# Attention weights times V on one core: register loops for the copying engines, and the last unit's product in two column parts

## The chip, the cores and the metric

One core of a Trainium2 chip. The metric is the device time of one execution in microseconds (us), median of the runs of a kernel. A profile's span is some 1.8 us shorter than the time of the same run (1057.4 against 1059.18 us for the kernel before), so spans are compared with spans and times with times.

## The reference

```python
# attn_weights: 8 x 12 x 1024 x 1024 float32, v: 8 x 12 x 1024 x 64 float32
np.einsum('bhqs,bhsd->bhqd', attn_weights, v).astype(np.float32)
```

96 heads, 403 MB of weights, each used once.

## The kernel before

The weights come in 48 *units* of 4 MB in bf16 (8 MB read in fp32: the page gives 427.82 MB read from HBM, which is the weights and V in fp32; a load writes `abf` in bf16, 4096 KB an issue). Units 0 to 45 hold half of each of four heads (a *quad*, two units); units 46 and 47 hold two heads each. In every unit TensorE transposes 16 groups `g` of weights into PSUM, VectorE and ScalarE copy them to `at`, TensorE multiplies them with V, and the product is copied to `ot`, transposed back, and copied to the output buffer. Two units are in flight (`abf[0]`, `abf[1]`); GpSimd queues a load as soon as the unit that held its buffer has been transposed. The stores of the last four full quads are held back until the last load has been queued (two of them, by GpSimd) or has landed (two, by SyncE).

TensorE runs a register loop already. VectorE and ScalarE are unrolled:

```python
            for n in range(NU):
                for g in range(G):
                    if on_dve(g) == dve:
                        eng.wait_ge(s_t[dve], n * per + count_of(g))
                        ins = copy(out=at[:, g]..., in_=bank[g % 4].bitcast(bf16))
                        # ... cut
                eng.wait_ge(s_m[e], n + 1)
                # ... cut
                copy(out=o, in_=x).then_inc(s_ot[e])
            back_copy(NU - 1, 1 - e).then_inc(s_fin[1 - e])
```

The last unit arrives in four quarters. The product of a pair of heads is done by row half: both heads of half 0, then both of half 1. Note where the wait for the last quarter stands:

```python
            for g in range(G):
                if g in starts:
                    pe.wait_ge(*s_piece[n, starts[g]])   # g == 12: the last quarter
                if t == 1 and g == 12:
                    wait_both(s_vbf, n + 1)
                    pair_half(t, 0)                      # needs groups 0 to 7 alone
                transpose_g(abf[t], g, n + 1)
                # ... cut
            for half in range(t, 2):
                pair_half(t, half)
        wait_both(s_ot, NU + 1)
        transpose_back()
```

## Time and profile before

| | before |
|---|---|
| time, median (lowest to highest) | 1059.76 us (1059.4 to 1059.97) |
| span of the profile | 1057.4 us |
| DMA share of a pair of units in mid-run (43.55 us) | 1.01 |
| VectorE, ScalarE busy in such a pair | 16.0, 16.4 us |
| landing of the last load to the end of the span | 17.5 us |

The prediction shows the lines behind these numbers: the slices, the windows of a pair of units, the chain of work in order of time, and the windows of the end. Two more lines of the page of before are from the table of DMA queues; the columns are packets, MB, and the share of 16 engines' span:

```profile
q8 instruction: 4, 0.07, 0.0%
q14 instruction: 10, 0.08, 0.0%
```

The page labels both *instruction*, and I take them for the transfers that bring code to the engines while the kernel runs. They are 14 in all, of 8 KB each in queue 14 (0.08 MB over 10) and 16 KB in queue 8 (0.07 MB over 4).

### The profile page before, as it was taken

The page shows a single profiled execution, that of the slowest core. Times are in us where ns is not written, and L with a number is a line of the kernel's source. Part 1 is how long each engine was busy: PE and PEld are TensorE (multiplying, and loading weights), DVE is VectorE, ACT ScalarE, POOL GpSimd, SP SyncE. Part 2 cuts the span into 40 slices and gives each one's busy share as a digit, 9 for nine tenths or more (in the row PEclk, how much of TensorE's full clock was granted, in tenths as well). Part 3 has the DMA queues.
Part 4 walks back from the last instruction along what each step waited for, and adds up shares of the span by engine and source line. Part 5 has one row for each costly group of instructions (what it writes and reads, how often), then busy time and mean ns, then how long its engine had stood idle before and what let it go on. Part 6 is the DMA issues. An engine that isn't in the chain of part 4 may idle for free.

```text
span 1057.4 us, 15231 instructions
## 1 busy us (share of the span) xinstructions
PE 756.6 (72%) x6856; PEld 703.3 (67%) x6856; DVE 387.6 (37%) x582; ACT 394.1 (37%) x480; POOL 54.0 (5%) x105
## 2 busy tenths in 40 slices
PE   0876686856877668776687677776767668676796
PEld 0776586756866667666677576775767658676784
DVE  1443343423443234333353333433344334332443
ACT  0443343433443234333343333433344334433453
POOL 1000000000000000000000000000000000000010
PEclk9988888988889788888898878888788888888899
DMA  9999999999999999999999999999999999999997
GB/s 218 219 219 208 243 232 218 234 210 240 238 218 238 216 238 238 218 236 226 223 236 214 237 236 217 238 218 238 237 218 238 205 242 238 213 215 217 217 212 251
DMA packets 14958, 239.75 MB, mean 227 GB/s; under 512 B 1632, under 2 KB 2144, under 8 KB 5216
## 3 DMA queue, kind: packets, MB, share of 16 engines
q0 software_dynamic: 13824, 235.41, 99.2%
q1 hardware_dynamic: 1120, 4.19, 1.0%
q8 instruction: 4, 0.07, 0.0%
q14 instruction: 10, 0.08, 0.0%
HBM read 427.82 MB, written 25.17 MB: 428 GB/s over the span
## 4 chain that ended last, share of the span: by engine, by line
DMA 76%; PE 22%; issue 1%; POOL 0%; DVE 0%; ACT 0%; POOLq 0%; SPq 0%
DMA abf<-in_attn_weights_dram 76%; PE bank L127 22%; PE bank L169 1%; POOL abf L328 0%; PE bank L154 0%; DVE at L286 0%; DVE osb_last L265 0%; ACT ot L306 0%; POOLq L427 0%; SPq L77 0%
## 5 line engine op out<-in xcount | busy, mean ns | idle before, releaser
L127 PE MATMUL bank<-ident,abf 128*128 128x128 f32 x3072 | 466.6, 325 | 262.0 <-DMA abf<-in_attn_weights_dram 261.9
L127 PEld LDWEIGHTS bank<-ident,abf 128*128 128x128 f32 x3072 | 457.1, 215 | 275.3 <-DMA abf<-in_attn_weights_dram 274.3
L286 DVE COPY at<-bank 128x1024 bf16<-128x1024 bf16 x480 | 319.8, 688 | 498.6 <-PE bank L127 497.1
L286 ACT COPY at<-bank 128x1024 bf16<-128x1024 bf16 x288 | 289.1, 1012 | 440.4 <-PE bank L127 440.4
L169 PE MATMUL bank<-at,vbf 128*64 128x256 bf16 (+1 forms) x3008 | 220.2, 280 | 2.1 <-DMA abf<-in_attn_weights_dram 1.3
L169 PEld LDWEIGHTS bank<-at,vbf 128*64 128x64 bf16 x3008 | 194.9, 108 | 21.8 <-DVE at L286 4.8
L306 ACT COPY ot<-bank 128x512 f32<-128x512 f32 x48 | 28.1, 585 | 184.5 <-PE bank L169 184.5
L306 DVE COPY ot<-bank 128x512 f32<-128x512 f32 x48 | 33.2, 691 | 152.2 <-PE bank L169 152.2
L154 PE MATMUL bank<-ident,ot 128*128 128x128 f32 x392 | 52.2, 276 | 31.6 <-DVE vbf L251 30.9
L328 POOL DMA_DIRECT2D abf<-in_attn_weights_dram x52 | 27.7, 533 | 896.2 <-PE bank L127 895.2
L154 PEld LDWEIGHTS bank<-ident,ot 128*128 128x128 f32 x392 | 43.3, 141 | 44.3 <-DVE vbf L251 42.2
L265 ACT COPY osb<-bank 128x512 f32<-128x512 f32 x92 | 49.4, 589 | 19.9 <-PE bank L154 19.9
L251 DVE CAST vbf<-bank 128x512 bf16<-128x512 f32 x48 | 31.0, 686 | 7.3 <-PE bank L142 7.3
L251 ACT CAST vbf<-bank 128x512 bf16<-128x512 f32 x48 | 25.9, 588 | 11.9 <-PE bank L142 11.9
L142 PE MATMUL bank<-vr,spread 32*128 32x512 bf16 x384 | 26.7, 377 | 0.0
L142 PEld LDWEIGHTS bank<-vr,spread 32*128 32x128 bf16 x384 | 10.2, 92 | 7.3
L340 POOL DMA_DIRECT2D out_dram<-osb x21 | 11.3, 540 | 41.7 <-ACT osb L265 41.7
L333 POOL DMA_DIRECT2D vr<-in_v_dram x23 | 12.1, 527 | 19.2 <-PE bank L142 18.9
L315 DVE CAST vr<-v 128x2048 bf16<-128x2048 f32 x1 | 1.5, 1498 | 3.2 <-DMA v<-in_v_dram 3.2
L361 POOL TENSOR_SCALAR_AFFINE_SELECT spread<-spread 32x512 bf16<-32x512 bf16 x4 | 2.5, 628 | 0.6
L265 ACT COPY osb_last<-bank 128x512 f32<-128x512 f32 x3 | 1.7, 587 | 0.8 <-PE bank L154 0.8
L265 DVE COPY osb_last<-bank 128x512 f32<-128x512 f32 x1 | 0.7, 690 | 2.9 <-PE bank L154 2.9
(9 smaller groups left out, 3.4 us busy)
## 6 DMA issues: line engine op xcount, KB each, us to landing
abf<-in_attn_weights_dram POOLq DMA_DIRECT2D x46, 4096.0 KB, 33.3
out_dram<-osb POOLq DMA_DIRECT2D x21, 1024.0 KB, 34.3
vr<-in_v_dram POOLq DMA_DIRECT2D x23, 512.0 KB, 34.5
abf<-in_attn_weights_dram POOLq DMA_DIRECT2D x2, 2048.0 KB, 26.3
abf<-in_attn_weights_dram POOLq DMA_DIRECT2D x4, 1024.0 KB, 22.9
out_dram<-osb SPq DMA_DIRECT2D x2, 1024.0 KB, 7.5
v<-in_v_dram SPq DMA_DIRECT2D x1, 1024.0 KB, 4.8
out_dram<-osb_last SPq DMA_DIRECT2D x1, 512.0 KB, 10.2
```

The source lines that it names most:

```text
L127: last = pe.matmul(out=pt[g % 4][:, k], lhsT=words[:, k], rhs=ident, is_transpose=True, start=(k == 0), stop=(k == KW - 1),)
L142: last = pe.matmul(out=ps, lhsT=spread[rows, b], rhs=vr[rows, b], start=(b == 0), stop=(b == VB - 1),)
L154: last = pe.matmul(out=px[k][:, ds(j * P, P)], lhsT=ot[:, 4 * k + j], rhs=ident, is_transpose=True, start=(j == 0), stop=(j == 3),)
L169: last = pe.matmul(out=outs, lhsT=vbf[:, 2 * kw + par, h], rhs=at[:, ds(half * GH, GH), kw, ds(col * np_, np_), par], start=(n == 0), stop ...
L251: copy(out=vbf[:, :, h], in_=ps.rearrange("p (k d) -> p k d", k=SB)).then_inc(s_vbf[e])
L265: return copy(out=halves[:, :, ds(4 * k, 4)].rearrange("p half j d -> p j half d"), in_=px[k].rearrange("p (j half d) -> p j half d", half ...
L286: ins = copy(out=at[:, g].rearrange("c k j two -> c (k j two)"), in_=bank[g % 4].bitcast(bf16),)
L306: copy(out=o, in_=x).then_inc(s_ot[e])
L328: pool.dma_start(out=abf[n % 2][:, ds(g0, gn)].rearrange("p g s -> p (g s)"), in_=in_).then_inc(s_abf[n % 2] if k == 0 else s_piece[n, k][ ...
L333: pool.dma_start(out=vr.rearrange("p b x -> p (b x)"), in_=v_g[iv]).then_inc(s_v, 16)
L340: eng.dma_start(out=out_q[q], in_=osb[q % NO].rearrange("p r d -> p (r d)"), **({} if by_sync else {"single_packet": True}),).then_inc(s_e ...
L361: pool.affine_select(out=spread[ds(h * VP, VP)], in_=spread[ds(h * VP, VP)], compare_op=mybir.AluOpType.not_equal, fill=1.0, base=0, patte ...
```

## The change

Its parts: (a) VectorE and ScalarE run register loops, of two and four units; (b) for these, the output buffers in the loop are two that alternate, and SyncE passes on to ScalarE, as `s_free`, which is free; (c) the products of the two last units are ordered by head, with the row half changing inside; (d) the last unit's product is done in two column parts (groups 0 to 3 and 8 to 11, then 4 to 7 and 12 to 15), each over both row halves, each transposed back and copied by itself; (e) the last quarter is loaded in two pieces, five loads in all. The diff, cut to its core:

```diff
-        NU - 1: [(0, 4), (4, 4), (8, 4), (12, 4)],
+        NU - 1: [(0, 4), (4, 4), (8, 4), (12, 2), (14, 2)],
 ...
-        def pair_half(t, half):
+        def multiply_pair(t, j0, jn):
             for h in range(2):
-                last = multiply(po[h][ds(half * D, D)], 2 * t + h, half, HP, h)
-                if half == 1:
-                    last.then_inc(s_m[h])
+                for half in range(2):
+                    outs = po[h][ds(half * D, D), ds(j0 * HP, jn * HP)]
+                    last = multiply(outs, 2 * t + h, half, HP, h, j0, jn)
+                last.then_inc(s_m[h])
 ...
+                if t == 1 and g == 12:
+                    wait_both(s_vbf, n + 1)
+                    wait_both(s_cp[10:12], n + 1)
+                    multiply_pair(t, 0, 4)
                 if g in starts:
                     pe.wait_ge(*s_piece[n, starts[g]])
-                if t == 1 and g == 12:
-                    wait_both(s_vbf, n + 1)
-                    pair_half(t, 0)
 ...
-        transpose_back()
+        transpose_back([(0, 4, px[0])])
+        wait_both(s_last, NU)
+        multiply_pair(1, 4, 4)
+        wait_both(s_ot, NU + 2)
+        transpose_back([(4, 2, px[1]), (6, 2, bank[0])])
 ...
-            for n in range(NU):
+            un, iters = (2, LOOPED) if dve else (4, BY_EIGHTS)
+            with nc.Fori(1, iters + 1, 1, engines=(DVE if dve else ACT,)) as it:
+                base = [eng.snap(it * (un * k) - un * k) for k in (per, 1, 2, 1)]
+                of_free = None if dve else eng.snap(it * 2 - 2)
+                for n in range(un):
+                    rows = osb[(n - 1) // 2 % 2][:, ds((n - 1) % 2 * G, G)]
+                    unit(n, base, rows, of_free + (n + 1) // 2 if n % 2 == 1 and not dve else None)
 ...
+            if 0 < q <= 2 * (BY_EIGHTS - 1):
+                nc.sync.wait_ge(s_osb[slot(q - 1)], 16 * ((q - 1) // 2 + 1))
+                nc.sync.sem_inc(s_free)
```

More of the change, by code (lines that the diff above doesn't have):

```diff
@@ L32 @@
     bf16 = mybir.dt.bfloat16
-    PE = mybir.EngineType.PE
+    PE, DVE, ACT = (getattr(mybir.EngineType, x) for x in ("PE", "DVE", "Activation"))
     B, H, Q, S = attn_weights.shape
@@ L54, with slot @@
     BY_SYNC = HELD_FROM + 2
-    NO = HELD + 2
+    BY_EIGHTS = HELD_FROM // 2
+    NO = 2 + LOOPED - 2 * BY_EIGHTS
     pieces_of = {
         NU - 2: [(0, GH), (GH, GH)],
-        NU - 1: [(0, 4), (4, 4), (8, 4), (12, 4)],
+        NU - 1: [(0, 4), (4, 4), (8, 4), (12, 2), (14, 2)],
     }
+    def slot(q):
+        return q % 2 if q < 2 * BY_EIGHTS else q - 2 * BY_EIGHTS + 2
     attn_q = attn_weights.rearrange("b (hq four) (p r) s -> (b hq) (four p) (r s)", four=VH, p=VP)
@@ L117 @@
         s_memset, s_const, s_vr = sem("s_memset"), sem("s_const"), sem("s_vr")
+        s_free = sem("s_free")
         pe = nc.tensor
@@ L149, in spread_v, with transpose_back @@
                 last.then_inc(s_sp[h % 2])
-        def transpose_back():
-            for k in range(2):
-                for j in range(4):
+        def transpose_back(parts=((0, 4, px[0]), (4, 4, px[1]))):
+            for j0, jn, ps in parts:
+                for j in range(jn):
                     last = pe.matmul(
-                        out=px[k][:, ds(j * P, P)],
-                        lhsT=ot[:, 4 * k + j],
+                        out=ps[:, ds(j * P, P)],
+                        lhsT=ot[:, j0 + j],
                         rhs=ident,
@@ L159, in transpose_back, with multiply @@
                         start=(j == 0),
-                        stop=(j == 3),
+                        stop=(j == jn - 1),
                     )
                 last.then_inc(s_back)
-        def multiply(outs, h, half, np_, col):
+        def multiply(outs, h, half, np_, col, j0=0, jn=GH):
             n = 0
@@ L171, in multiply @@
                         lhsT=vbf[:, 2 * kw + par, h],
-                        rhs=at[:, ds(half * GH, GH), kw, ds(col * np_, np_), par],
+                        rhs=at[:, ds(half * GH + j0, jn), kw, ds(col * np_, np_), par],
                         start=(n == 0),
@@ L232 @@
                 wait_both(s_vbf, n + 1)
-            wait_both(s_last, n + 1)
-            for half in range(t, 2):
-                pair_half(t, half)
+                wait_both(s_last, n + 1)
+                multiply_pair(t, 0, GH)
         wait_both(s_ot, NU + 1)
-        transpose_back()
+        transpose_back([(0, 4, px[0])])
[3 more added lines that the diff above has]
+        transpose_back([(4, 2, px[1]), (6, 2, bank[0])])
         def engine(dve):
@@ L244, in engine, with spread_copy @@
             e = 0 if dve else 1
-            spreads = 0
-            def spread_copy(h, ps):
-                nonlocal spreads
-                spreads += 1
-                eng.wait_ge(s_sp[e], spreads)
+            def spread_copy(h, ps, count):
+                eng.wait_ge(s_sp[e], count)
                 copy(
@@ L253, in spread_copy @@
                 ).then_inc(s_vbf[e])
-            def back_copy(n, k):
-                if n < NU - 2:
-                    if n % 2 == 0 and k == 0 and n // 2 >= NO:
-                        eng.wait_ge(s_osb[n // 2 % NO], 16 * (n // 2 // NO))
-                    rows = osb[n // 2 % NO][:, ds(n % 2 * G, G)]
-                else:
-                    rows = osb_last[n % 2]
-                halves = rows.rearrange("p (half j) d -> p half j d", half=2)
-                eng.wait_ge(s_back, 2 * (n + 1) + k + 1)
-                return copy(
-                    out=halves[:, :, ds(4 * k, 4)].rearrange("p half j d -> p j half d"),
-                    in_=px[k].rearrange("p (j half d) -> p j half d", half=2, d=D),
-                )
@@ L270, in middle @@
-            def middle(n):
-                if n < NU - 2:
-                    if n % 2 == 0:
-                        spread_copy(e, po[e])
-                        spread_copy(2 + e, px[e])
-                else:
-                    spread_copy(2 * (n % 2) + e, po[e])
-                if not dve and n > 0:
-                    back_copy(n - 1, 0)
-                    back_copy(n - 1, 1).then_inc(s_out)
-            for n in range(NU):
-                for g in range(G):
-                    if on_dve(g) == dve:
-                        eng.wait_ge(s_t[dve], n * per + count_of(g))
-                        ins = copy(
-                            out=at[:, g].rearrange("c k j two -> c (k j two)"),
-                            in_=bank[g % 4].bitcast(bf16),
-                        )
-                        if g < G - 4:
-                            ins.then_inc(s_cp[g])
-                        elif g == (G - 1 if dve else G - 2):
-                            ins.then_inc(s_last[e])
-                    if g == 3 and n == NU - 1:
-                        middle(n)
-                if n < NU - 1:
-                    middle(n)
-                eng.wait_ge(s_m[e], n + 1)
-                if n < NU - 2:
-                    o = ot.rearrange("c j (h p) -> c h j p", h=VH)[:, ds(2 * e, 2)]
-                    x = po[e].rearrange("c (h j p) -> c h j p", h=2, j=GH)
-                else:
-                    o = ot.rearrange("c j (h p) -> c h j p", h=2)[:, e]
-                    x = po[e].rearrange("c (j p) -> c j p", j=GH)
-                copy(out=o, in_=x).then_inc(s_ot[e])
@@ L307, in engine, with back_copy, rows_of @@
-            back_copy(NU - 1, 1 - e).then_inc(s_fin[1 - e])
+            def back_copy(rows, j0, jn, ps, count):
+                eng.wait_ge(s_back, count)
+                return copy(
+                    out=rows.rearrange("p (half j) d -> p j half d", half=2)[:, ds(j0, jn)],
+                    in_=ps[:, ds(0, jn * P)].rearrange("p (j half d) -> p j half d", half=2, d=D),
+                )
+            def rows_of(n):
+                if n < NU - 2:
+                    return osb[slot(n // 2)][:, ds(n % 2 * G, G)]
+                return osb_last[n % 2]
@@ new lines, in back_copies, with copy_g @@
+            def back_copies(rows, count, free=None):
+                if free is not None:
+                    eng.wait_ge(s_free, free)
+                for k in range(2):
+                    last = back_copy(rows, 4 * k, 4, px[k], count + k + 1)
+                last.then_inc(s_out)
+            def copy_g(g, count):
+                eng.wait_ge(s_t[dve], count)
+                ins = copy(
+                    out=at[:, g].rearrange("c k j two -> c (k j two)"),
+                    in_=bank[g % 4].bitcast(bf16),
+                )
+                if g < G - 4:
+                    ins.then_inc(s_cp[g])
+                elif g == (G - 1 if dve else G - 2):
+                    ins.then_inc(s_last[e])
@@ new lines, in product_four, with product_pair @@
+            def product_four(count):
+                eng.wait_ge(s_m[e], count)
+                copy(
+                    out=ot.rearrange("c j (h p) -> c h j p", h=VH)[:, ds(2 * e, 2)],
+                    in_=po[e].rearrange("c (h j p) -> c h j p", h=2, j=GH),
+                ).then_inc(s_ot[e])
+            def product_pair(j0, jn, count):
+                eng.wait_ge(s_m[e], count)
+                copy(
+                    out=ot.rearrange("c j (h p) -> c h j p", h=2)[:, e, ds(j0, jn)],
+                    in_=po[e].rearrange("c (j p) -> c j p", j=GH)[:, ds(j0, jn)],
+                ).then_inc(s_ot[e])
@@ new lines, in engine, with unit @@
+            mine = [g for g in range(G) if on_dve(g) == dve]
+            def unit(n, base, rows, free):
+                of_t, of_sp, of_back, of_m = base
+                for g in mine:
+                    copy_g(g, of_t + (n * per + count_of(g)))
+                if n % 2 == 0:
+                    spread_copy(e, po[e], of_sp + (n + 1))
+                    spread_copy(2 + e, px[e], of_sp + (n + 2))
+                if not dve:
+                    back_copies(rows, of_back + 2 * n, free)
+                product_four(of_m + (n + 1))
@@ new lines, in engine @@
+            for n in range(un * iters, NU - 2):
+                unit(n, (0, 0, 0, 0), rows_of(n - 1), None)
+            for t in range(2):
+                n = NU - 2 + t
+                for g in mine:
+                    if t == 1 and g >= 12 and mine[mine.index(g) - 1] < 12:
+                        product_pair(0, 4, n + 1)
+                    copy_g(g, n * per + count_of(g))
+                    last = mine[-1] if t == 0 else [x for x in mine if x < 4][-1]
+                    if g == last:
+                        spread_copy(2 * t + e, po[e], n + 1)
+                        if not dve:
+                            back_copies(rows_of(n - 1), 2 * n)
+                if t == 0:
+                    product_pair(0, GH, n + 1)
@@ L309 @@
+            if not dve:
+                back_copy(rows_of(NU - 1), 0, 4, px[0], 2 * NU + 1).then_inc(s_fin[0])
+            product_pair(4, 4, NU + 1)
+            ps = px[1] if dve else bank[0]
+            back_copy(rows_of(NU - 1), 4 + 2 * e, 2, ps, 2 * NU + 2 + e).then_inc(s_fin[1])
         nc.vector.memset(ident, 0.0).then_inc(s_memset)
@@ L338, in store @@
             eng = nc.sync if by_sync else pool
-            eng.wait_ge(s_out, 2 * q + 2)
+            eng.wait_ge(s_out, 2 * q + 3)
             eng.dma_start(
                 out=out_q[q],
-                in_=osb[q % NO].rearrange("p r d -> p (r d)"),
+                in_=osb[slot(q)].rearrange("p r d -> p (r d)"),
                 **({} if by_sync else {"single_packet": True}),
-            ).then_inc(s_end if by_sync else s_osb[q % NO], 16)
+            ).then_inc(s_end if by_sync else s_osb[slot(q)], 16)
         load_attn(0)
@@ L385 @@
         nc.sync.dma_start(out=v32.rearrange("p b x -> p (b x)"), in_=v_g[0]).then_inc(s_v0, 16)
-        for iv in range(1, NV):
-            nc.sync.wait_ge(s_v, 16 * iv)
+        nc.sync.sem_inc(s_free, 2)
+        for q in range(LOOPED):
+            nc.sync.wait_ge(s_v, 16 * (q + 1))
             nc.sync.sem_inc(s_vr)
+            if 0 < q <= 2 * (BY_EIGHTS - 1):
+                nc.sync.wait_ge(s_osb[slot(q - 1)], 16 * ((q - 1) // 2 + 1))
+                nc.sync.sem_inc(s_free)
         nc.sync.wait_ge(*s_piece[NU - 1, len(pieces_of[NU - 1]) - 1])
@@ L391 @@
             store(q, by_sync=True)
-        nc.sync.wait_ge(s_out, NU - 1)
+        nc.sync.wait_ge(s_out, NU)
         nc.sync.dma_start(out=out_p[NU - 2], in_=osb_last[0]).then_inc(s_end, 16)
         for k in range(2):
-            nc.sync.wait_ge(s_fin[k], 1)
+            nc.sync.wait_ge(s_fin[k], k + 1)
             gs = [x.rearrange("p (half g) d -> p half g d", half=2)[:, :, ds(4 * k, 4)]
@@ L398 @@
             nc.sync.dma_start(out=gs[0], in_=gs[1]).then_inc(s_end, 16)
-        for q in range(BY_SYNC - NO, BY_SYNC):
-            nc.sync.wait_ge(s_osb[q % NO], 16 * (q // NO + 1))
+        for q in range(2 * BY_EIGHTS - 2, BY_SYNC):
+            nc.sync.wait_ge(s_osb[slot(q)], 16 * BY_EIGHTS if q < 2 * BY_EIGHTS else 16)
         nc.sync.wait_ge(s_end, 16 * (LOOPED - BY_SYNC + 3))
```

## The prediction

> **What bounds the kernel now.** I read the page's slices and queue table first, then the chain of work in order of time, then windows of 43.55 us, then the timeline and the windows of the last 50 us.
>
> ```profile
> DMA  9999999999999999999999999999999999999997
> ...
> q0 software_dynamic: 13824, 235.41, 99.2%
> ...
> DMA 76%; PE 22%; issue 1%; POOL 0%; DVE 0%; ACT 0%; POOLq 0%; SPq 0%
> ```
>
> The first line is the mean busy share of the 16 DMA engines: 90% or more in every slice but the last. The second says that the queue of the loads alone fills 99.2% of the engines' span. The third, the chain that ended last, gives TensorE 22%, which looks like something to win. The windows, one for each pair of units, say it is not:
>
> ```profile
> 524.40:567.95 43.55, 31.64 (x290) 29.76 (x289) 16.02 (x24) 16.39 (x20) 2.12 (x4) 0.85 1.01 229
> ```
>
> In 43.55 us (two units) VectorE is busy 16.02 us, ScalarE 16.39 us, TensorE 31.64 us, and the DMA share is 1.01. The compute part of the chain is work beside a transfer already queued:
>
> ```profile
> 509.00 0.53 POOL L328 DMA_DIRECT2D abf<-in_attn_weights_dram  x1 [17.77 <-PE bank L127]
> ...
> 523.85 6.35 PE L127 MATMUL bank<-ident,abf 128*128 128x128 f32 x30 [7.30 <-DMA abf<-in_attn_weights_dram]
> ```
>
> The next load was queued at 509.00 and the one before it landed only at 523.85: transposes and copies could run some 15 us late before the DMA queue ran dry. So from about 2 us to the landing of the last load the time is bytes over DMA rate, and only the end can be won. The chain there:
>
> ```profile
> 1010.48 29.42 DMA abf<-in_attn_weights_dram
> 1039.94 3.80 PE bank L169 x16
> 1043.74 2.15 PE bank L127 x16
> 1045.91 0.70 DVE at L286
> 1046.66 3.81 PE bank L169 x16
> 1050.49 0.59 ACT ot L306
> 1051.09 0.14 issue
> 1051.22 1.08 PE bank L154 x8
> 1052.33 0.69 DVE osb_last L265
> ```
>
> The last quarter of the last unit lands at 1039.9. Only then does TensorE do the product of the first row half (3.80 us), which needs nothing of that quarter: it stands behind the wait in program order. Then come 16 transposes, a copy, the product of the second half, copy, transpose back, copy. The last two stores are issued at 1052.50 and 1053.15, and the span ends at 1057.4. From landing to end: 17.5 us.
>
> [...] in the timeline
>
> ```profile
> 1009.43 4.48 PE L169 MATMUL bank<-at,vbf 128*64 128x256 bf16 x64
> ...
> 1012.00 0.69 DVE L306 COPY ot<-bank 128x512 f32<-128x512 f32 x1 [2.65 <-PE bank L169]
> ...
> 1024.04 6.55 PE L169 MATMUL bank<-at,vbf 128*64 128x512 bf16 x32
> ```
>
> 64 products of 256 columns that change the column half every 8 take 4.48 us (70 ns each), while 32 of 512 columns, the same columns, that stay 16 long on one half take 6.55 us. Changing halves often is worth a third. [...]
>
> **The change, part by part.** *Register loops on VectorE and ScalarE.* They replace unrolled copies by the same copies with waits on registers: nearly one register operation for each of some 18 or 19 instructions a unit, and one branch for 2 units (VectorE) or 4 (ScalarE). [...] Two additional copies back in unit 0 (0.59 us each on ScalarE) also lie under the loads. Before the last two units nothing changes in bytes, in their order, or in how many stores are held back (2 issued by GpSimd, 2 by SyncE): 0 us.
>
> *Buffers of the output.* Two alternate in the loop in place of six. ScalarE now waits for the store of two quads (four heads) earlier. A store is issued about 10 us after a quad's first unit starts and lands after 34.3 us; its buffer is asked for some 65 us after that issue: 30 us to spare, 0 us.
>
> *Product of the last but one unit.* The order of its four runs of 8 now changes the half each time, 32 of 512 columns. The loop's pattern took 2.57 us (1009.43 to 1012.00) for 32 of 256, so about 5.1 us in place of 6.55: TensorE is free 1.4 us earlier, at 1029.1.
>
> *The last unit.* Its four loads were issued at 1008.92 to 1010.48 and landed after 16.4 to 29.4 us: 1025.3, 1030.2, 1035.0 and 1039.9, one each 4.87 us. The fourth becomes two: 1037.4 and, with all bytes the same, 1039.9 again. Groups 4 to 11 follow 1.4 us earlier (group 8 just meets its load at 1035.0), and the last copy of them ends at 1038.2 in place of 1039.65. The first column product no longer waits for a load: 1038.2 + 2.5 = 1040.7. Transposes of groups 12 to 15 start there; from their start to their last copy it was 2.93 us (1043.67 to 1046.60), so 1043.6. The four first transposes back fit in that gap. Second column product: 2.57 us to ScalarE's copy, 1046.2. That copy has 256 columns: ScalarE's 0.585 us for 512 and 1.01 for 1024 extrapolate to 0.37 (estimate), 1046.6. Then 0.15 of waiting, two and two transposes back and a copy of 256 columns, about 0.67 + 0.37: 1047.8. The last store is issued then, not at 1053.15: **the compute end moves by 5.3 us**: 3.8 of it are the product that no longer follows the landing, the rest the shorter product and copies, less a first column product that now delays groups 12 to 15 by 0.8.
>
> *What the stores make of it.* The other end does not move. Behind the last load stand four held stores of 1 MB and one of 0.5 MB:
>
> ```profile
> 1046.00:1048.00 2.00, 1.34 (x6) 0.68 (x7) 0.60 (x1) 0.44 (x1) 0.00 (x0) 1.00 0.97 406
> 1048.00:1050.00 2.00, 2.00 (x10) 0.97 (x9) 0.69 (x1) 0.00 (x0) 0.00 (x0) 1.00 0.32 131
> 1050.00:1052.00 2.00, 1.23 (x10) 0.81 (x8) 0.00 (x0) 0.70 (x2) 0.00 (x0) 1.00 0.02 8
> ```
>
> ```profile
> out_dram<-osb_last SPq DMA_DIRECT2D x1, 512.0 KB, 10.2
> out_dram<-osb_last SPq DMA_DIRECT2D x2, 256.0 KB, 2.6
> ```
>
> The last two numbers of each window are DMA share and GB/s: full until 1048, a few slow engines until 1050.4. The 512 KB store, issued at 1040.8, lands at 1051.0. In the old kernel the last two stores came to idle engines. In the new one they are ready at about 1044.3 and 1047.8 and stand behind that backlog. On the slowest engines it grows by both: they took 1.55 us together (1053.75 to 1055.3), so data end at about 1050.4 + 1.5 = 1051.9. From data end to the span's end it was 2.1 us: 1054.0. The compute path alone would give 1047.8 + 4.2 = 1052.0. The later counts: 1057.4 − 1054.0 = 3.4 us, and I take 3.7[...]. The time is then 1059.7 − 3.7 = **1056.0 us**.
>
> **Rivals.** *The compute end is the bound, and stores hide:* 1059.7 − 5.4 = 1054.3. For it: the mean backlog is gone by 1048.3, and only two or three engines are late. Against it: a store is done when its slowest engine is. *The loops hurt:* a late copy delays the transposes, these the loads. For it: waits on registers and a jump back at each turn. Against it: 15 us of slack and 37% busy engines. If a stall of a few us fell on each turn, still 0; only over 15 us would it show, as DMA shares below 0.95 in the 43.55 us windows, 1060 or more. *The output buffers stall:* with two in the loop, a store later by 30 us would stop ScalarE and then TensorE; each such stall costs what it exceeds the slack by; nothing in the landing times (34.0 median, 36.1 at most) points there. *Code fetch:* shorter programs for two engines save transfers, but the queues of kind instruction hold 14 packets, 0.15 MB of 239.75: below 0.6 us.
>
> **Range and chances.** The two ends give 1054.3 and 1056.3; half a us for landings, and more if the five loads slow the last landing or the two column products overlap less than in the loop: 1054.0 to 1057.8. Two per cent are 21 us, more than the whole end of 17.5: faster 0.01, same 0.98, slower 0.01.
>
> **What would show it.** In the new profile: DMA share still 1.00 and 43.55 us a pair in mid-run; the last load's landing near 1039.9; the first column product near 1038.2, before that landing; the second starting at 1043.6 and taking 2.5 us, not 3.8; the last store issued near 1047.8 with a landing of 4 us or so, not 2.6, if the backlog holds it, and about 2.6 if the compute end is the bound. Wrong would be: a pair longer than 43.6 us, ScalarE waiting for free output buffers, or a last landing moved by over 1 us.

What no trace of this case shows is cut from the recorded text, with the cuts marked; the part on the order of the matmuls therefore begins in mid-sentence. The sum came to 1059.7 − 3.7 = 1056.0 us: 0 for the loops, 0 for the buffers, 3.7 for the end. And the reason for taking 3.7 where 3.4 was worked out is gone; the 0.3 was my estimate, which no run shows. That a store is done when its slowest engine is, the profile of before shows: the 512 KB store lands at 1051.0, 2.7 us after the 1048.3 at which the prediction has the mean backlog gone, and in the last half us in which anything moves (1050.0 to 1050.5) the DMA share is 0.08.

## The result, and the profile after

1055.41 us median of 4 runs (1054.98 to 1056.07), against 1059.76 before: 4.35 us less; ratio 0.996, 95% interval 0.9943 to 0.9977. That is "the same" at 2%, clear of noise, and inside the predicted range.

The chain of work of the changed kernel in order of time, from unit 46's product on (columns: start us, us, what):

```profile
1023.84 4.74 PE bank L176 x32
...
1038.03 2.52 PE bank L176 x32
1040.56 2.13 PE bank L134 x16
...
1042.71 0.70 DVE at L287
...
1043.46 2.57 PE bank L176 x32
...
1046.05 0.38 ACT ot L306
...
1046.56 0.64 PE bank L161 x4
...
1047.23 0.37 ACT osb_last L268
```

There is no load in this part of the chain any more: compute is done at 1047.60, where the old kernel was done at 1053.02. That is 5.4 us, but the span is only 3.7 us shorter (1053.7 against 1057.4). The windows of the end show where the rest went. The columns are busy time by engine, granted clock, DMA share and GB/s, as in the three windows of before:

```profile
1046.00:1048.00 2.00, 0.64 (x5) 0.42 (x4) 0.42 (x1) 0.74 (x2) 0.00 (x0) 1.00 0.98 408
1048.00:1050.00 2.00, 0.00 (x0) 0.00 (x0) 0.00 (x0) 0.00 (x0) 0.00 (x0) 1.00 0.95 353
1050.00:1052.00 2.00, 0.00 (x0) 0.00 (x0) 0.00 (x0) 0.00 (x0) 0.00 (x0) 0.90 0.17 58
```

Every compute engine is idle from 1048 on, and the DMA engines are full until 1050 (share 0.95, where it was 0.32 before). The end has become a drain of stores. SyncE's timeline and its waits say the same from the other side:

```profile
1039.59 0.82 SPq L385 DMA_DIRECT2D out_dram<-osb  x2
...
1043.76 4.40 SPq L447 DMA_DIRECT2D out_dram<-osb_last  x2
```

```profile
SPq L450 <- DMA out_dram<-osb_last: 3.7, 1, 3.7
```

The first issue comes on the landing of the last load, at 1039.59. The last two stores are issued from 1043.76 on, the second one's issue ends at 1048.16, and SyncE then waits 3.7 us for the stores to land; in the old kernel that wait was 1.9 us:

```profile
SPq L401 <- DMA out_dram<-osb_last: 1.9, 1, 1.9
```

In mid-run nothing moved. The window of the same pair of units as before, and two lines of the page:

```profile
524.40:567.95 43.55, 31.22 (x290) 29.35 (x289) 16.02 (x24) 17.62 (x21) 2.12 (x4) 0.85 1.01 229
```

```profile
q14 instruction: 4, 0.03, 0.0%
...
L287 ACT ACT_TABLE_LOAD x9 | 11.5, 1283 | 1.2 <-SPq L83 1.1
```

The DMA share is 1.01 again, and VectorE has the same 16.02 us. ScalarE has 1.28 us more in every other pair: its function table is now loaded inside the loop, nine times, where the unrolled kernel loaded it once. And the code transfers in queue 14 fell from 10 to 4.

### The profile page after: what moved, and what is told of

Read it like the earlier page. It is cut to its first block, busy times and chain, and to the rows that moved or that the text cites. A ratio compares the mean times of both kernels' runs of the same rounds, so it can differ in the third digit from the quotient of the medians.

```text
span 1053.7 us, 16145 instructions
## 1 busy us (share of the span) xinstructions
PE 753.2 (71%) x6888; PEld 704.7 (67%) x6888; DVE 387.5 (37%) x583; ACT 404.9 (38%) x492; POOL 54.6 (5%) x106
## 4 chain that ended last, share of the span: by engine, by line
DMA 73%; PE 25%; issue 1%; ACT 0%; DVE 0%; POOL 0%; POOLq 0%; SPq 0%
DMA abf<-in_attn_weights_dram 73%; PE bank L134 23%; PE bank L176 1%; PE bank L161 0%; ACT at L287 0%; PE bank L149 0%; DVE at L287 0%; POOL abf L373 0%; ACT ot L306 0%; ACT osb_last L268 0%; POOLq L476 0%; SPq L83 0%
## 5 line engine op out<-in xcount | busy, mean ns | idle before, releaser
L176 PE MATMUL bank<-at,vbf 128*64 128x256 bf16 x3040 | 215.9, 279 | 1.5 <-ACT at L287 1.2
L268 ACT COPY osb<-bank 128x512 f32<-128x512 f32 x94 | 50.5, 589 | 20.8 <-PE bank L161 20.8
L287 ACT ACT_TABLE_LOAD x9 | 11.5, 1283 | 1.2 <-SPq L83 1.1
```

Source lines behind the costliest of these rows:

```text
L176: last = pe.matmul(out=outs, lhsT=vbf[:, 2 * kw + par, h], rhs=at[:, ds(half * GH + j0, jn), kw, ds(col * np_, np_), par], start=(n == 0), ...
L268: return copy(out=rows.rearrange("p (half j) d -> p j half d", half=2)[:, ds(j0, jn)], in_=ps[:, ds(0, jn * P)].rearrange("p (j half d) -> ...
L287: ins = copy(out=at[:, g].rearrange("c k j two -> c (k j two)"), in_=bank[g % 4].bitcast(bf16),)
```

## The experiments

All are timed beside the kernel before on the same chip; the last column is the median of the runs of before recorded with it less the run's own. E1 to e4 ran on one chip, c0 and e5 to e11 on another. "Changed kernel" is the one above, the *control* is its repetition c0_after. All are "the same" at 2% but e11, which is slower (ratio 1.0289).

| run | what | median us (range) | less than before |
|---|---|---|---|
| c0_after | the changed kernel again | 1055.68 (1055.4 to 1056.36) | 4.28 |
| e1_tail_only | new end alone | 1056.52 (1056.0 to 1057.2) | 3.11 |
| e2_loops_only | loops and buffers alone | 1058.95 (1058.84 to 1059.17) | 0.68 |
| e3_hoist | before, one wait moved | 1058.24 (1057.85 to 1058.47) | 1.39 |
| e4_four_loads | four loads, not five | 1055.55 (1055.18 to 1055.99) | 4.08 |
| e5_delay6 | six copies ahead of the last one | 1055.63 (1055.28 to 1055.96) | 4.33 |
| e6_delay11 | eleven copies ahead of it | 1058.37 (1057.93 to 1058.5) | 1.59 |
| e7_no_held | no held stores (wrong result) | 1053.45 (1053.35 to 1054.41) | 6.51 |
| e8_held5 | five held stores | 1055.82 (1055.29 to 1056.44) | 4.01 |
| e9_held3 | three held stores | 1056.21 (1055.9 to 1056.45) | 3.62 |
| e10_half_order | products in the old order | 1056.46 (1056.22 to 1056.86) | 3.37 |
| e11_pad | more code on SyncE | 1089.53 (1085.0 to 1093.52) | −29.7 |

**The change in two.** The new end without loops:

```diff
-            with nc.Fori(1, iters + 1, 1, engines=(DVE if dve else ACT,)) as it:
-                ...
+            for n in range(NU - 2):
+                ...    # the copies of before, unrolled
-    NO = 2 + LOOPED - 2 * BY_EIGHTS
+    NO = HELD + 2
```

> The changed kernel without the register loops and with the six output buffers of before: only the new end (column parts, order of the last-but-one product, five loads). My theory, that the loops and buffers are worth nothing and the end everything: 1055.4 us as the changed kernel, within 0.5. Rival, that the shorter programs of VectorE and ScalarE give part of the gain: 1056 to 1058 us.

The loops with the old end:

```diff
-        NU - 1: [(0, 4), (4, 4), (8, 4), (12, 2), (14, 2)],
+        NU - 1: [(0, 4), (4, 4), (8, 4), (12, 4)],
-                multiply_pair(...)
+                pair_half(...)     # and the rest of the end of before
```

> The register loops and the two alternating output buffers, with the end of before (four loads, products by row half). My theory: 1059.7 us as before, within 0.4, although the loop of ScalarE loads its function table 9 times (11.5 us in the changed kernel's profile). Rival, that loops cost or give something: 1058 or less, or 1061 or more.

The end alone gave 3.11 us, the loops and buffers alone 0.68. My theory ("worth nothing") missed both by more than it allowed; the loops and buffers do give a part, whatever its cause: all five runs of e1 are slower than all five of e4 (the changed kernel with four loads), by 0.97 in the median though by only 0.01 at the edges, and all five of e2 are faster than all nine of before. The interval of e2's ratio (0.998 to 1.0007) still holds 1, so e2 by itself would not settle it. The two parts sum to 3.8 us, against 4.1 for e4 and 4.3 for the control; what is left is inside the scatter of the changed kernel's own runs (1054.98 to 1056.36).

**One moved wait.** The smallest edit that takes the old product from behind the landing:

```diff
-                if g in starts:
-                    pe.wait_ge(*s_piece[n, starts[g]])
                 if t == 1 and g == 12:
                     wait_both(s_vbf, n + 1)
                     pair_half(t, 0)
+                if g in starts:
+                    pe.wait_ge(*s_piece[n, starts[g]])
```

> The kernel before with one edit: the product of the first row half stands ahead of the wait for the last quarter, not behind it. It can start at 1038.65, when the transposes of groups 8 to 11 end, in place of 1039.94, so the rest follows 1.3 us earlier; before, the stores had drained by 1050.4, so the compute end sets the time there: 1059.7 - 1.3 = 1058.4 us. If the 3.8 us of that product were all behind the landing for the wait alone: 1056 us.

1.39 us, as expected. In its timeline the product starts before the landing, which SyncE's issue marks:

```profile
1039.16 3.80 PE L169 MATMUL bank<-at,vbf 128*64 128x512 bf16 x16
...
1040.54 0.82 SPq L340 DMA_DIRECT2D out_dram<-osb  x2
```

The wait itself is thus worth 1.4 us: TensorE had only that much free time before the landing. The rest of the product's 3.8 us still holds up the last transposes.

**Four loads.**

```diff
-        NU - 1: [(0, 4), (4, 4), (8, 4), (12, 2), (14, 2)],
+        NU - 1: [(0, 4), (4, 4), (8, 4), (12, 4)],
```

> The changed kernel with the last quarter of the last unit as one load in place of two. TensorE is busy with the first column product until 1040.6, later than the landing of the last load at 1039.6, so the extra load releases nothing sooner: 1055.4 us, within 0.4. Rival, that the smaller last load matters for the end: 1056.5 to 1057.8 us (up to 2.4 us later transposes).

1055.55 us: the fifth load does nothing that the scatter lets one see. TensorE is at the first column product until 1040.56, and by then (1039.59) all of the last quarter is there anyway.

**Is the end really set by the stores?** Copies from PSUM to a spare buffer delay ScalarE's last copy:

```diff
             product_pair(4, 4, NU + 1)
+            if not dve:
+                for i in range(6):          # 11 in e6_delay11
+                    copy(out=spare[:, i], in_=px[0])
```

> The changed kernel again, unaltered, beside the delays that follow on the same chip: 1055.4 us within 0.5 by every theory.

> The changed kernel with six extra copies of 512 columns on ScalarE ahead of its last copy, some 0.49 us each, so the last store is issued about 2.1 us later (1049.7 in place of 1047.6). My theory, that the backlog of held stores sets the end (its data end at 1051.7): the late store still meets the end of the backlog, 0 to +0.5 us. Rival, that the compute end sets the time: +2.1 us.

> The same with eleven extra copies: the last store is issued about 4.5 us later, at 1052.1, after the backlog. My theory: it goes out alone, issue 0.65 and data 0.75 us, data end about 1053.5 in place of 1051.7: +1.5 to +2 us. Rival (compute end): +4.5 us.

ScalarE's timeline and SyncE's wait with six copies:

```profile
1046.66 3.04 ACT L354 CAST spare<-bank 128x512 bf16<-128x512 f32 x6
...
1049.52 0.46 ACT L269 COPY osb_last<-bank 128x256 f32<-128x256 f32 x1
```

```profile
SPq L454 <- DMA out_dram<-osb_last: 1.8, 1, 1.8
```

The landing of the last load differs by up to 0.9 us between profiles of the same program (1039.6 in the first one of the changed kernel, 1040.5 in the control's), so the delay is best counted from it: the last copy starts 9.6 us after it with six copies, 12.0 with eleven, and 7.7 in both profiles without. That is 2.0 and 4.3 us later. With six copies the time is that of the control (1055.63 against 1055.68), and the wait for the stores shrank from 3.7 to 1.8 us instead. With eleven the delay passes the backlog, and the time rises by 2.7 us, not by 4.3. So the compute end had 1.6 to 2 us to spare. The 2.7 is more than the 1.5 to 2 us expected: in the trace of e6 the last store's data end 1.56 us after its issue does (1053.16 to 1054.72), where I had counted 0.75.

The opposite, no backlog:

```diff
-        for q in range(HELD_FROM, BY_SYNC):
-            store(q)
-        for q in range(BY_SYNC, LOOPED):
-            store(q, by_sync=True)
```

> The changed kernel without its four held stores of 1 MB at the end, so its result is wrong on purpose (four quads of heads are not written). No backlog: the last store, issued at 1047.65, finds idle engines. My theory: data end about 1049.1, the time 2.6 us lower than the changed kernel, about 1052.8 us. Rival (compute end sets the time already): no change, 1055.4 us.

2.2 us faster than the control (1053.45 against 1055.68), close to the 2.6 expected, although compute ends where it did (1048.51 in its profile, 1048.52 in the control's). In its windows the engines are nearly empty when the last store comes:

```profile
1048.00:1050.00 2.00, 0.10 (x1) 0.00 (x0) 0.34 (x1) 0.37 (x1) 0.00 (x0) 0.84 0.13 44
```

The share is 0.13 where the changed kernel has 0.95. The result is wrong: four quads are not written. It is a measure, not a version to use.

**Moving the last landing.**

```diff
-    HELD = 4
+    HELD = 5        # 3 in e9_held3
```

> The changed kernel with five held stores in place of four: the last load lands some 2.4 us earlier (1 MB at 422 GB/s), and so does the compute end, but the engines have the same bytes to move. My theory (stores drain last): no change, within 0.5 us of 1055.4. Rival (compute end): 2.4 us faster, 1053.0.

> The changed kernel with three held stores: last load and compute end some 2.4 us later, last store issued about 1050.1, just when the backlog ends. My theory: 0 to +0.6 us. Rival (compute end): +2.4 us, 1057.8.

With five held stores the second column product starts at 1041.55, with three at 1046.38, against 1043.46: the compute end moved by −1.9 and +2.9 us in the profiles (−2.8 and +2.0 against the control's). The gain over before moved from 4.28 to 4.01 and 3.62 us. A compute end that sets the time would have given gains near 6.2 or 7.1 with five, and 1.4 or 2.3 with three. So what sets it is the whole of the bytes, loads and stores together, however the held stores divide them; with three, the compute end comes up to the edge that e6 found, and 0.7 us is lost.

**The order of the products.**

```diff
-            for h in range(2):
-                for half in range(2):
+            for half in range(2):
+                for h in range(2):
```

> The changed kernel with its three last products in the order of before: both heads of one row half, then of the other, so the column half of the array changes once in 32 matmuls and not three times. The last-but-one product should take 6.55 us again in place of 4.81, and each column product about 3.3 in place of 2.53. The compute end is then up to 3.2 us later; by my theory the backlog hides most of it: 0 to +0.8 us. By the rival +3 us. If the order did not matter on the array, the products would keep their 4.81 and 2.53 us.

The timeline has them as expected, 6.54 us for unit 46's product and 3.37 for a column part, in place of 4.81 and 2.52:

```profile
1023.35 6.54 PE L176 MATMUL bank<-at,vbf 128*64 128x512 bf16 x32
...
1039.04 3.37 PE L176 MATMUL bank<-at,vbf 128*64 128x256 bf16 x32 [1.20 <-ACT at L288]
```

The same matmuls take a quarter less time when the column half of the array changes after every eight. The edit also changes how often the PSUM bank changes; the starts of the single matmuls in the traces tell the two apart. In unit 46's product of e10 matmuls start about 226 ns apart, also where the bank alone changes (after 8 and after 24). Only around the one change of half are there four pairs, the two of a pair 6 to 34 ns apart. The changed kernel has four such pairs at each of its three changes of half, two of which stay in one bank. So it is the half. The last copy starts at 1049.93, 2.7 us later (3.0 counted from the last landing), and the gain over before falls by 0.9 us (4.28 to 3.37): the backlog hid two thirds of the delay.

**What does fetching code cost?** The loops' 0.7 us had no place in my account. The changed kernel has six code transfers fewer than before, so the last run multiplies these, on an engine that has nothing to do (SyncE waits for the loads of V for 978.4 of the 1053.7 us):

```diff
                 nc.sync.sem_inc(s_free)
+            if q < LOOPED - 1:
+                for _ in range(768):
+                    nc.sync.wait_ge(s_v0, 16)
```

> The changed kernel with a longer program on SyncE: after each pair of units, 768 waits that are already met[...], at a time when SyncE has nothing to do. It asks what fetching code costs. In the profiles the fetches during the run took 0.32 us of one DMA engine each, 10 of them in the kernels with unrolled copies and 4 in those with loops, and the loops alone measured 0.7 us faster. Theory: a fetch delays one engine of a saturated set, and loads end with the slowest engine: 66 more fetches of 8 KB are 21 us of engine time, so +1.3 us if they spread evenly over 16 engines, more if they fall unevenly, up to +21 us on one. Rival, that fetches cost nothing and the 0.7 us had another cause: 1055.6 us, within 0.5.

The page:

```profile
q14 instruction: 70, 0.57, 0.1%
```

66 transfers more, 0.5 MB of 240, and 33.9 us more than the changed kernel (1089.53 against 1055.68 in the control, another call with the same kernel before). The count of 66 was expected; the page gives 70 against 4, 24 KB for each of 22 pairs. The trace records 16 increments of its semaphore for each load, as many as there are DMA engines, and not at one time: those of unit 22 in the changed kernel spread over 2.5 us, and TensorE starts on the unit at 499.79, just after the last of them (499.75). I take each increment for one engine's share; that is my reading, since the trace kept here names no engine. So how far the slowest engine lags the median can be worked out for each load (last increment minus median, and second last minus median), in us, for every second unit from unit 6 on:

```
changed kernel  slowest  1.78 1.78 1.78 1.78 1.81 1.82 1.80 1.80 1.82
                second   1.65 1.65 1.66 1.66 1.65 1.65 1.65 1.64 1.65
e11_pad         slowest  2.00 3.09 4.04 5.06 5.92 6.88 7.77 8.72 9.67
                second   1.16 1.41 1.41 1.42 1.49 1.49 1.43 1.43 1.43
```

The last increment falls behind by 0.96 us a pair (2.00 to 9.67 in eight), and the second last does not (1.41 to 1.49 from the second column on). Three transfers of 8 KB were added per pair, and the trace gives each 0.322 us: 0.97. So, by that reading, SyncE's code comes over one DMA engine, and in this stretch that engine does not catch up. Unit 22 lands 7.9 us later than in the changed kernel (507.6 against 499.7), all of it this engine's: the median increments are at 497.95 and 497.93. Neither the even spread (+1.3) nor the rival (nothing) fits; the unevenness does. What stays open: 66 × 0.322 is 21 us, the most that the theory allowed, and 34 were lost. From about 525 us on the lag wavers between 9 and 16 us, and the rate falls from 229 to between 226 and 187 GB/s in the windows of 43.55 us, although the DMA share stays within 0.99 to 1.01 in all but one (0.90). Why more is lost than the fetches themselves take was not tried.

The same measure tests whether the six avoided fetches are the loops' 0.7 us. Lag of the slowest engine, worked out from the kept traces, in us; the last column counts the transfers of queue 14 up to unit 44:

```
unit               5    12    22    30    44   transfers
before          1.68  1.87  1.81  1.82  1.88   9
e1_tail_only    1.91  1.91  2.60  2.60  2.60   9
e2_loops_only   2.16  2.17  2.12  2.12  2.12   2
changed kernel  1.78  1.78  1.82  1.78  1.76   2
c0_after        1.84  1.84  2.04  2.69  2.79   2
```

The kernels with fewer transfers don't have the smaller lag. In before, seven transfers came between units 10 and 44 and left the slowest engine where it was (1.87 and 1.88 us at units 12 and 44); what they did to the others the last increment does not show. And the control gained 0.65 us of lag between units 22 and 23, when neither queue moved any code: lags of this size have another source too, which no run here shows. The control's profile, with 1.0 us more lag than the first one of the changed kernel, has a span 0.9 us longer. So the traces don't support fetches as the cause of the 0.7 us; single profiles can't exclude them either.

## Why the prediction was right or wrong

*DMA is the bound until the last landing; loops in 15 us of slack.* Right as to compute: DMA share 1.01 in mid-run, ScalarE even carries 11.5 us of table loads without harm, and a register operation took 35 to 63 ns. The branch of a loop took 50 to 63 ns on VectorE and 40 to 50 on ScalarE:

```profile
L327 DVEq COMPARE_BRANCH  x23: 50/56/63, 57.7 to 1012.1; - x23
...
L327 ACTq COMPARE_BRANCH  x9: 40/45/50, 102.5 to 800.2; - x9
```

The output buffers did not stall: all that ScalarE waited for before its copies into them was TensorE (20.8 us in total, 19.9 before).

*Code fetch "below 0.6 us", and "0 us" for the loops and the buffers.* The zero is the step that failed: together they measured 0.7 to 1.0 us (e2; e1 against e4). The cause stays open. Loops and buffers were not separated, and avoided fetches, the obvious candidate, are not borne out by the lags above. The reasoning behind "below 0.6", bytes over all 16 engines (0.15 of 239.75 MB, which is 0.66 of 1057 us), was wrong in kind: for SyncE's code e11 shows that a fetch costs its whole length on one engine (by the reading above, 0.96 us a pair for three of 0.322). Of fetches at the turns of the loops nothing is seen: 23 turns on VectorE and 9 on ScalarE, and 4 transfers in queue 14 in the whole run.

*Compute end moves by 5.3 us to 1047.8.* Right: 1047.60, 5.4 us. Step by step, predicted and measured: TensorE free of unit 46 at 1029.1 and 1028.58; first column product at 1038.2 and 1038.03; last transposes at 1040.7 and 1040.56; their last copy done at 1043.6 and 1043.41; second product to copy 2.57 and 2.59 us; copy of 256 columns 0.37 and 0.37. The pattern taken from the loop's own products (changing halves every eight) carried over, and e10 shows that it is the order that does it.

*Stores become the end, data until 1051.9, span end 1054.0.* The mechanism is right: e5, e7, e8 and e9 exclude the rival that the compute end is the bound, and e6 finds the edge about 2 us later. The span ended at 1053.7. As a size, the end was worked out at 3.4 us, taken as 3.7 (the 0.3 by an estimate that no run shows), and measured 3.1 by itself (e1). Whether slow engines catch up on the last stores no run isolates; from load to load, in the table of lags above, the slowest one does not. Single profiles don't split the remaining 0.6 us: the last landing was at 1040.68 in that of e1 and at 1039.59 in the changed kernel's, but at 1040.50 in that of the control, which is the same program; the lag of the slowest engine at unit 44 is 2.6, 1.8 and 2.8 us in these three.

*The first product that waits for nothing.* The prediction gave 3.8 of the 5.3 us to the product that no longer follows the landing, less 0.8. Moving the wait alone gave 1.4 (e3): without the shorter products ahead of it TensorE has no more room. The sum was right, the label too simple.

*The total.* 1056.0 predicted, 1055.41 measured: the end 0.6 us too large, the loops 0.7 to 1.0 too small. Two misses that partly cancel: that the total came out so close is partly luck.

## What to carry to other kernels

When one resource is full from start to end, take the last transfer's landing and list what stands behind it on each side, compute and transfers; the later of the two sets the time, and a delay of a known size put on purpose into one of them tells which it is. Before adding smaller loads, ask whether the engine that uses them will be free then: here a moved product and the order of matmuls did the work, and the fifth load none. In a DMA-bound kernel look at the last of the 16 increments of a load, not at the mean share: in e11, with 66 more code transfers, the last increment fell behind by 0.96 us a pair from unit 6 to unit 22, and the share of the windows until then still read 1.00 to 1.02. That a few transfers fewer are felt is not shown here.
